# Banks of a product opened one by one, and queries and keys 2 and 3 made in one product

## The chip, the cores and the metric

The kernel runs on one core of one Trainium2 chip. The metric is the device time of one execution in microseconds. Three runs of the kernel before gave 1106.72 to 1108.7 us with a median of 1107.58 us; less is better.

## The reference

A trunk of two layers on 512 tokens of width 1024, in float32. Layer A mixes with trailing means, layer B with twelve heads of stick-breaking attention, and both have four memory heads beside that and a SwiGLU block behind. Layer B's queries, and the keys and values, are projections of the same x, with two different gains in front of the matrices.

```python
D_MODEL, SEQ, DEPTH = 1024, 512, 2            # BATCH = 1
HEAD_DIM, N_SB_HEADS, N_MEM_HEADS, MEM_TOKENS = 64, 12, 4, 256
D_FF, SB_BLOCK = 2816, 128

def stick_breaking_attention(q, k, v):
    ...
    for i in range(s // SB_BLOCK):
        ...
        z = jnp.einsum("bhqd,bhkd->bhqk", qb, kb).astype(jnp.float32) * scale
        mask = spos[None, :] < tpos[:, None]
        log_not = jnp.where(mask, jax.nn.log_sigmoid(-z), 0.0)
        later = lax.cumsum(log_not, axis=3, reverse=True) - log_not
        wts = jnp.where(mask, jnp.exp(jax.nn.log_sigmoid(z) + later), 0.0)
        outs.append(jnp.einsum("bhqk,bhkd->bhqd", wts.astype(vb.dtype), vb))

def pool_layer(x, mem, ...):                  # layer A
    proj = rmsnorm(x, norm_mix) @ w_in
    u_pool, q_mem = proj[..., :POOL_WIDTH], proj[..., POOL_WIDTH:]
    ...                                       # trailing means, grouped matmul
    mem_out = memory_attention(q_mem, mk, mv)
    x = x + jnp.concatenate([grouped, mem_out], axis=-1) @ w_out
    return x + swiglu(rmsnorm(x, norm_ffn), w_gu, w_down)

def sb_layer(x, mem, k_sh, v_sh, ...):        # layer B
    proj = rmsnorm(x, norm_mix) @ w_q         # 12 heads of queries, 4 memory heads
    ...
    sb_out = stick_breaking_attention(q_sb, k_sh, v_sh)...
    mk, mv = memory_kv(mem, mem_norm, w_mem_kv)
    mem_out = memory_attention(q_mem, mk, mv)
    x = x + jnp.concatenate([sb_out, mem_out], axis=-1) @ w_out
    return x + swiglu(rmsnorm(x, norm_ffn), w_gu, w_down)

# in reference(): before layer B
            kv = rmsnorm(x, kv_norm) @ w_kv   # keys and values from the same x, another gain
# at the end
    return rmsnorm(x, final_norm)
```

## The kernel before

**Tiles and products.** x stands as 8 tiles of 128 features by 512 tokens. Each float32 operand of a product is split in a high and a low part (h and l at the end of a name), and a product of two operands is three matmuls: low part with high, high with low, and high with high (`mm3`, L278 to L280). Weights are cut in bricks of 128 rows by up to 512 columns. SyncE loads two bricks with one transfer of 512 KB (names `wr_...`), into a ring of four. `wsplit` makes the high part on ScalarE (L223, or L227 with a gain) and the low part on VectorE (L224, or L228 with a gain); these too have a ring of four, and run two bricks ahead. A gain belongs to a range of columns, so a brick whose columns come from two matrices with different gains is split in as many pieces, each with its own instruction on either engine.

**Banks.** A product collects four outputs (n) of 128x512 in four banks of PSUM ("acc"); four more ("at") serve the attention heads. `product` runs the bricks (k) over the banks. `staggered` sets the order: brick by brick over all banks, and at the end, for the last two bricks (`STAGGER`), bank by bank, so that the banks close one after another. A bank opens when what read the product before out of it is done.

**Layer B's queries, keys and values.** They are made by five products, `b_qkv0` to `b_qkv4`, whose outputs `QKV_GROUPS` lists (L82): q 6 and 7 are the memory heads' queries, each other q or k holds two of the twelve heads, each v four heads. When a bank closes, `evac` in `qkv` reads it out. For a q, `stack_q` makes the high part (ScalarE, L237) and the low part (VectorE, L238), and four transfers on SyncE's queue (L505) bring them into the tiles `qs` that the scores read. For a k, VectorE first multiplies with the row scale (`qkf`, L978), ScalarE makes the high part (`hk`, L513), VectorE the low part (L514), and `dup_k` issues eight transfers. `qh`, `ql`, `qkf` and `hk` share one ring of four buffers (tag "hl"), so a fifth of them waits until the transfers that read the first are done. For a v, ScalarE (L551) and VectorE (L552) write it token by token.

**Attention.** A head and block of tokens starts with scores `zs` on TensorE (L610, L611), then two sigmoids on ScalarE (`nb`, `be`; L613, L614), masks on GpSimd (L615, L617), a scan (`it`, L620) and a multiplication (`be`, L622) on VectorE. TensorE transposes the weights (`tp`, L561), ScalarE and VectorE split them (`ath`, `atl`; L237, L238, or a copy on ScalarE alone for the later heads, L565), and TensorE multiplies with the values (`av`, L650). Memory heads run through `zm`, `pt` and the same transposes. A head can begin when its q and its k have been brought in place.

**What sets the order.** TensorE's order is written by hand by a planner in the program: it keeps a clock of its own, charges each engine for what it issues (`chain`, `COST`), notes when each tile will be there, and weaves pieces of heads between a product's steps where it expects them to be ready. The other engines' order follows from a scheduler that sees TensorE's. Each engine runs its instructions in order, so an instruction that waits holds up all that is behind it.

Of the kernel before, what the change touches and what calls it, by code (L numbers as in the profile page):

```python
# [59 lines left out]
STAGGER = 2  # L60
# [18 lines left out]
POOL_LEAD = 1.32  # L79
MAN_A = True  # L80
MAN_B = True
QKV_GROUPS = [[('q', 6), ('q', 7), ('q', 0), ('q', 1)], [('k', 0), ('k', 1), ('v', 0)], [('q', 2), ('q', 3), ('q', 4), ('q', 5)], [('k', 2), ('k', 3), ('v', 1)], [('k', 4), ('k', 5), ('v', 2)]]  # L82


def _plan():
# [3 lines left out]
    def ffn(l, g):  # L89
        out = []  # L90
        for (j0, j1), downs in PARTS[l]:
            for _ in range(j0, j1, 2):
                out.append((f"{l}_gu", k8, [(0, 512, g)]))
            for d0, d1 in downs:
                out += [(f"{l}_down", list(range(d0, d1)), None)] * 2
        if l == "b":
            out.append(("b_last", list(range(*LAST)) * 2, None))
        return out
# [11 lines left out]
    plan += ffn("a", G_AFFN)  # L110
    for gi, tiles in enumerate(QKV_GROUPS):
        cuts, c = [], 0
# [13 lines left out]
class Net:  # L126
# [85 lines left out]
    def wsplit(self, w, k, gains=None, stays=False):  # L212

        nc = self.nc
        cols = w.shape[-1]
        self.chain([("act", cols), ("dve", cols)] if gains is None else [("acts", cols), ("stt", cols)])
        if stays:
            wh, wl = self.t("xh", F32R), self.t("xl", F32R)
        else:
            wh = self.wp.tile([P, cols], F32R, tag="wh", name="wh", bufs=4)  # L220
            wl = self.wp.tile([P, cols], F32R, tag="wl", name="wl", bufs=4)
        if gains is None:
            nc.scalar.copy(wh, w)  # L223
            nc.vector.tensor_tensor(out=wl, in0=w, in1=wh.bitcast(F32), op=ALU.subtract)  # L224
        else:
            for c0, c1, g in gains:
                nc.scalar.activation(wh[:, c0:c1], w[:, c0:c1], AF.Copy, scale=self.gain(g, k))  # L227
                nc.vector.scalar_tensor_tensor(  # L228
                    out=wl[:, c0:c1], in0=w[:, c0:c1], scalar=self.gain(g, k),
                    in1=wh.bitcast(F32)[:, c0:c1], op0=ALU.mult, op1=ALU.subtract)  # L230
        return wh, wl
# [127 lines left out]
    def product(self, name, ks, nb, mul, evac, alone=False):  # L359

        ps = [self.any_ps("acc") if alone else self.ps("acc", "acc") for _ in range(nb)]
        w = {}
        for i, n in staggered(len(ks), nb):
            if i not in w:
                w[i] = self.next_brick(name)
            if i == 0 and not alone:
                self.until(self.accs.popleft())
            mul(ps[n], n, *w[i], ks[i], i == 0, i == len(ks) - 1)
            if i == len(ks) - 1:
                done = evac(n, ps[n])  # L370
                if not alone:
                    self.accs.append(done)
            yield
# [299 lines left out]

def staggered(nk, nb):

    for k in range(nk - STAGGER):
        for n in range(nb):
            yield k, n
    for n in range(nb):
        for k in range(nk - STAGGER, nk):  # L680
            yield k, n
# [8 lines left out]
def trunk_kernel(ctx: ExitStack, tc: tile.TileContext, a, out):  # L690
# [274 lines left out]
    def qkv(gi):  # L965
        tiles = QKV_GROUPS[gi]
        units = [u for u, (t, _) in enumerate(tiles) for _ in range(1 + (t == "v"))]
# [74 lines left out]
    with net.in_order() if MAN_B else ExitStack():  # L1042
        for gi in range(len(QKV_GROUPS)):
            net.weave(qkv(gi), ma, att)
# [80 lines left out]
```

## Time and profile before

| what | us |
|---|---|
| median of three runs | 1107.58 |
| the profiled execution | 1108.93 |
| its span | 1107.2 |
| TensorE busy | 1086.5 |
| VectorE busy | 679.2 |
| ScalarE busy | 498.4 |
| GpSimd busy | 77.1 |

The profile is taken from one execution. TensorE's busy time is the length of its matmuls, which overlap: one of 512 columns is listed with about 390 ns, and the next starts 0.23 us after it. So the end of a wait is read better from the starts of two neighbours than from the busy time. The chain that ended last is 90% TensorE's own instructions.

### The profile page before, as it was taken

What the parts mean: (1) busy time and instruction counts of PE and PEld (TensorE: products, weight loads), DVE (VectorE), ACT (ScalarE), POOL (GpSimd) and SP (SyncE); (2) the same over time, 40 slices, a digit from 0 to 9 for tenths busy, and PEclk for the clock granted to TensorE, in tenths of its full rate; (3) what the DMA queues carried; (4) which work ended last, traced back from release to release, by engine and by line L of the source; (5) the groups of instructions that cost most, each with busy time, mean ns of one, the idle gap of its engine ahead of it and who ended that gap; (6) DMA issues with size and microseconds to landing.
All of it is one profiled execution on the core that took longest, in us unless ns stands there. A gap on an engine that the chain in (4) does not pass through costs nothing.

```text
span 1107.2 us, 14396 instructions
## 1 busy us (share of the span) xinstructions
PE 1086.5 (98%) x5280; PEld 913.4 (82%) x5280; DVE 679.2 (61%) x1118; ACT 498.4 (45%) x911; POOL 77.1 (7%) x130
## 2 busy tenths in 40 slices
PE   9999999999999999999998999999999999999997
PEld 7997888888888888888877888788888888888887
DVE  7987876544444534565578799784653365444574
ACT  7557553332333323344786676553332243323343
POOL 0000040000000000000013133240000000000000
PEclk9999999999999999999999999999999999999998
DMA  7464222222222222223554433122222222222212
GB/s 269 141 198 122 76 96 95 95 95 95 96 97 104 99 100 96 95 95 102 145 135 125 124 110 107 52 85 87 95 104 104 96 96 96 96 95 95 96 57 77
DMA packets 39366, 117.48 MB, mean 106 GB/s; under 512 B 5120, under 2 KB 7168, under 8 KB 39296
## 3 DMA queue, kind: packets, MB, share of 16 engines
q1 hardware_dynamic: 39152, 116.54, 32.0%
q8 instruction: 41, 0.67, 0.2%
q14 instruction: 29, 0.24, 0.1%
q10 hardware_dynamic: 144, 0.03, 0.0%
HBM read 100.83 MB, written 2.10 MB: 93 GB/s over the span
## 4 chain that ended last, share of the span: by engine, by line
PE 90%; issue 4%; ACT 2%; DVE 1%; DMA 1%; POOL 1%; SPq 0%; POOLq 0%; DVEq 0%; ACTq 0%
PE acc L278 27%; PE acc L279 27%; PE acc L280 27%; PE av L650 2%; PE tp L561 1%; ACT pt L592 1%; DMA wr_a_in<-in_a_in_dram 1%; PE zs L610 1%; PE zs L611 1%; PE ps_ss L302 0%; PE last L278 0%; PE last L279 0%; DMA qs<-ql 0%; ACT wh L227 0%; POOL be L617 0%
## 5 line engine op out<-in xcount | busy, mean ns | idle before, releaser
L278 PE MATMUL acc<-xh,wh 128*128 128x512 f32 x880 | 342.9, 392 | 1.7 <-DVE vs L552 1.1
L279 PE MATMUL acc<-xl,wh 128*128 128x512 f32 x880 | 342.8, 390 | 0.0
L280 PE MATMUL acc<-xh,wl 128*128 128x512 f32 x880 | 341.8, 389 | 0.0
L278 PEld LDWEIGHTS acc<-xh,wh 128*128 128x128 f32 x880 | 165.6, 188 | 35.7 <-issue 1.5
L280 PEld LDWEIGHTS acc<-xh,wl 128*128 128x128 f32 x880 | 165.2, 188 | 34.6
L279 PEld LDWEIGHTS acc<-xl,wh 128*128 128x128 f32 x880 | 165.4, 188 | 32.9 <-DVE xl L238 0.2
L228 DVE SCALAR_TENSOR_TENSOR wl<-wr_a_gu,gains,wh 128x512 fp32r<-128x512 f32 x88 | 67.1, 766 | 105.7 <-ACT wh L227 105.7
L228 DVE SCALAR_TENSOR_TENSOR wl<-wr_b_gu,gains,wh 128x512 fp32r<-128x512 f32 x88 | 67.0, 762 | 105.6 <-ACT wh L227 105.6
L278 PE MATMUL acc<-hh,wh 128*128 128x512 f32 x320 | 124.5, 389 | 0.0
L279 PE MATMUL acc<-hl,wh 128*128 128x512 f32 x320 | 124.5, 389 | 0.0
L280 PE MATMUL acc<-hh,wl 128*128 128x512 f32 x320 | 124.3, 389 | 0.0
L227 ACT ACTIVATE wh<-wr_b_gu,gains 128x512 fp32r<-128x512 f32 x88 | 63.6, 724 | 133.5 <-PE acc L279 105.5
L227 ACT ACTIVATE wh<-wr_a_gu,gains 128x512 fp32r<-128x512 f32 x88 | 63.3, 724 | 133.3 <-PE acc L279 107.3
L278 PEld LDWEIGHTS acc<-hh,wh 128*128 128x128 f32 x320 | 60.1, 188 | 12.5
L280 PEld LDWEIGHTS acc<-hh,wl 128*128 128x128 f32 x320 | 60.1, 188 | 12.5
L279 PEld LDWEIGHTS acc<-hl,wh 128*128 128x128 f32 x320 | 60.1, 188 | 12.4
L224 DVE TENSOR_TENSOR wl<-wr_a_down,wh 128x512 fp32r<-128x512 f32 x44 | 30.4, 690 | 60.1 <-ACT wh L223 49.9
L223 ACT CAST wh<-wr_a_down 128x512 fp32r<-128x512 f32 x44 | 27.4, 622 | 72.6 <-PE acc L279 67.9
L307 POOL TENSOR_TENSOR rs<-var,mhalf 128x4 f32<-128x4 f32 (+1 forms) x7 | 6.6, 942 | 756.1 <-DVE var L305 756.1
L224 DVE TENSOR_TENSOR wl<-wr_b_down,wh 128x512 fp32r<-128x512 f32 x36 | 24.9, 690 | 49.1 <-ACT wh L223 40.9
L278 PE MATMUL acc<-mixh,wh 128*128 128x512 f32 x128 | 51.6, 403 | 2.8 <-DVE mixl L860 1.5
L279 PE MATMUL acc<-mixl,wh 128*128 128x512 f32 x128 | 50.2, 392 | 0.2 <-DVE mixl L1020 0.2
(204 smaller groups left out, 1691.4 us busy)
## 6 DMA issues: line engine op xcount, KB each, us to landing
wr_a_gu<-in_a_gu_dram SPq DMA_DIRECT2D x44, 512.0 KB, 3.5
wr_b_gu<-in_b_gu_dram SPq DMA_DIRECT2D x44, 512.0 KB, 3.5
wr_a_down<-in_a_down_dram SPq DMA_DIRECT2D x22, 512.0 KB, 3.5
wr_b_qkv<-in_b_qkv_dram SPq DMA_DIRECT2D x20, 512.0 KB, 3.6
wr_b_down<-in_b_down_dram SPq DMA_DIRECT2D x18, 512.0 KB, 3.5
wr_a_out<-in_a_out_dram SPq DMA_DIRECT2D x8, 512.0 KB, 3.5
wr_b_out<-in_b_out_dram SPq DMA_DIRECT2D x8, 512.0 KB, 3.6
wr_a_in<-in_a_in_dram SPq DMA_DIRECT2D x7, 512.0 KB, 4.0
```

Of the source, the lines that this page charges most:

```text
L223: nc.scalar.copy(wh, w)
L224: nc.vector.tensor_tensor(out=wl, in0=w, in1=wh.bitcast(F32), op=ALU.subtract)
L227: nc.scalar.activation(wh[:, c0:c1], w[:, c0:c1], AF.Copy, scale=self.gain(g, k))
L228: nc.vector.scalar_tensor_tensor(out=wl[:, c0:c1], in0=w[:, c0:c1], scalar=self.gain(g, k), in1=wh.bitcast(F32)[:, c0:c1], op0=ALU.mult, o ...
L278: mm(ps, wh, xh, start=first, stop=False)
L279: mm(ps, wh, xl, start=False, stop=False)
L280: mm(ps, wl, xh, start=False, stop=last)
L561: nc.tensor.transpose(tp[:, i * P:(i + 1) * P], blk, self.ident)
L592: nc.scalar.activation(pt[:, b], z[:, b], AF.Exp, scale=sp[:, 2 * pr + i:2 * pr + i + 1], bias=mx[:, i:i + 1], accum_out=sm[:, i:i + 1])
L610: nc.tensor.matmul(z[:, :end], q, kh[:, :end], start=True, stop=False)
L611: nc.tensor.matmul(z[:, :end], q, kl[:, :end], start=False, stop=True)
L650: self.nc.tensor.matmul(to, vv, part, start=ia == 0 and i == 0, stop=ia == nu - 1 and i == len(parts) - 1)
```

## The change

`QKV_GROUPS` puts k 2 and 3 with q 2 and 3 in the third product, and q 4 and 5 with v 1 in the fourth. `wsplit` charges the planner's clock for each piece of a brick. `staggered` begins a product of more than four bricks (`2 * STAGGER`) bank by bank with the first two bricks, in the way in which it ended before. This holds for both layers' input products but the very first of the program, the q, k and v products, and the longer part of each output product; the SwiGLU block has an order of its own.

```diff
--- before.py
+++ after.py
@@ -79,7 +79,7 @@
 POOL_LEAD = 1.32
 MAN_A = True
 MAN_B = True
-QKV_GROUPS = [[('q', 6), ('q', 7), ('q', 0), ('q', 1)], [('k', 0), ('k', 1), ('v', 0)], [('q', 2), ('q', 3), ('q', 4), ('q', 5)], [('k', 2), ('k', 3), ('v', 1)], [('k', 4), ('k', 5), ('v', 2)]]
+QKV_GROUPS = [[('q', 6), ('q', 7), ('q', 0), ('q', 1)], [('k', 0), ('k', 1), ('v', 0)], [('q', 2), ('q', 3), ('k', 2), ('k', 3)], [('q', 4), ('q', 5), ('v', 1)], [('k', 4), ('k', 5), ('v', 2)]]
 
 
 def _plan():
@@ -213,7 +213,8 @@
 
         nc = self.nc
         cols = w.shape[-1]
-        self.chain([("act", cols), ("dve", cols)] if gains is None else [("acts", cols), ("stt", cols)])
+        for n in [None] if gains is None else [c1 - c0 for c0, c1, _ in gains]:
+            self.chain([("act", cols), ("dve", cols)] if n is None else [("acts", n), ("stt", n)])
         if stays:
             wh, wl = self.t("xh", F32R), self.t("xl", F32R)
         else:
@@ -673,7 +674,11 @@
 
 def staggered(nk, nb):
 
-    for k in range(nk - STAGGER):
+    first = STAGGER if nk > 2 * STAGGER else 0
+    for n in range(nb):
+        for k in range(first):
+            yield k, n
+    for k in range(first, nk - STAGGER):
         for n in range(nb):
             yield k, n
     for n in range(nb):
```

Bricks of the third and of the fourth product now have columns of two gains, so ScalarE runs 898 instructions in place of 882 in its listing and VectorE 1136 in place of 1120; TensorE, GpSimd and SyncE have as many as before.

Below are pieces of the order of instructions before and after, with the number of a tile or buffer behind its name; the lines of the changed file are one higher from L214 on, and five higher from L679 on.

TensorE at the opening of the third product. `acc_4970` to `acc_4973` are its four banks before, `acc_4974` to `acc_4977` after; `wh_4818` is brick 0, `wh_4843` and `wh_4845` brick 1. Of each step of three matmuls the first stands here. Before:

```order
L278 MATMUL acc_4970<-xh_4200,wh_4818 128x512
...
L561 MATMUL tp_4998<-ident_69,pt_4789 128x128 x2
...
L278 MATMUL acc_4971<-xh_4200,wh_4818 128x512
...
L278 MATMUL acc_4972<-xh_4200,wh_4818 128x512
...
L278 MATMUL acc_4973<-xh_4200,wh_4818 128x512
...
L278 MATMUL acc_4970<-xh_4207,wh_4843 128x512
...
L278 MATMUL acc_4971<-xh_4207,wh_4843 128x512
```

After:

```order
L279 MATMUL acc_4974<-xh_4200,wh_4818 128x512
...
L279 MATMUL acc_4974<-xh_4207,wh_4845 128x512
...
L562 MATMUL tp_5013<-ident_69,pt_4789 128x128 x2
...
L279 MATMUL acc_4975<-xh_4200,wh_4818 128x512
...
L279 MATMUL acc_4975<-xh_4207,wh_4845 128x512
...
L279 MATMUL acc_4976<-xh_4200,wh_4818 128x512
...
L279 MATMUL acc_4976<-xh_4207,wh_4845 128x512
...
L279 MATMUL acc_4977<-xh_4200,wh_4818 128x512
```

Banks 1, 2 and 3 open one, two and three steps later, and brick 1 is read by the second step in place of the fifth.

VectorE where the third product's outputs are read out. Before, `ql_5310` and `ql_5340` are the low parts of q3 and q4, and `atl_5387` is a slice of attention weights that TensorE's `zs` at 595.20 us came behind:

```order
L238 TENSOR_TENSOR ql_5310<-acc_4971,qh_5309 128x512
L622 TENSOR_TENSOR be_5295<-be_5295,it_5303 128x511
L620 SCALAR_TENSOR_TENSOR it_5330<-nb_5323 128x128
L238 TENSOR_TENSOR ql_5340<-acc_4972,qh_5339 128x512
L228 SCALAR_TENSOR_TENSOR wl_5372<-wr_b_qkv3_1_5369,gains_67,wh_5371 128x512
L622 TENSOR_TENSOR be_5322<-be_5322,it_5330 128x127
L228 SCALAR_TENSOR_TENSOR wl_5440<-wr_b_qkv3_1_5369,gains_67,wh_5439 128x512
L238 TENSOR_TENSOR atl_5387<-tp_5383,ath_5386 128x256
```

After, `qkf_5345` is k2 times the row scale, and `atl_5325` is the next slice:

```order
L239 TENSOR_TENSOR atl_5317<-tp_5311,ath_5316 128x512
L983 TENSOR_TENSOR qkf_5345<-acc_4976,rb_4509 128x512
L621 SCALAR_TENSOR_TENSOR it_5339<-nb_5332 128x512
L239 TENSOR_TENSOR atl_5325<-tp_5320,ath_5324 128x384
L229 SCALAR_TENSOR_TENSOR wl_5408<-wr_b_qkv3_1_5405,gains_67,wh_5407 128x256 x2
L623 TENSOR_TENSOR be_5331<-be_5331,it_5339 128x511
```

The row that needs the first buffer of the ring a second time is now a multiplication on VectorE, ahead of the scan and of the slice, and the weight splits are two halves each.

ScalarE in the same place. Before, `qh_5339` and `qh_5355` are the high parts of q4 and q5, `ath_5386` the high part of the slice:

```order
L237 CAST qh_5339<-acc_4972 128x512
L227 ACTIVATE wh_5371<-wr_b_qkv3_1_5369,gains_67 128x512
L227 ACTIVATE wh_5439<-wr_b_qkv3_1_5369,gains_67 128x512
L237 CAST qh_5355<-acc_4973 128x512
L237 CAST ath_5386<-tp_5383 128x256
```

After, `hk_5347` is k2's high part, and `ath_5324` and `ath_5436` are slices:

```order
L238 CAST ath_5324<-tp_5320 128x384
L228 ACTIVATE wh_5407<-wr_b_qkv3_1_5405,gains_67 128x256 x2
L614 ACTIVATE nb_5370<-zs_5366,sn_4476 128x128
...
L228 ACTIVATE wh_5416<-wr_b_qkv3_1_5405,gains_67 128x256 x2
L514 CAST hk_5347<-qkf_5345 128x512
L238 CAST ath_5436<-tp_5433 128x256
```

The weight splits now stand ahead of the row that waits for a buffer, and one slice does too.

## Rows read from the trace of the kernel before

**Rows 1.** The page, part 1: busy us (share of span) xinstructions, by engine.
```profile
PE 1086.5 (98%) x5280; PEld 913.4 (82%) x5280; DVE 679.2 (61%) x1118; ACT 498.4 (45%) x911; POOL 77.1 (7%) x130
```

**Rows 2.** TensorE's waits, 526.5 to 727.7 us: total us, times, longest us.
```profile
PE zs L610 <- DVE atl L238: 3.1, 1, 3.1
PE acc L278 <- DVE vs L552: 2.4, 3, 1.1
PE av L650 <- ACT ath L565: 1.2, 3, 0.4
```

**Rows 3.** Windows by stage: length, busy us of PE, PEld, DVE, ACT, POOL, PEclk, DMA, GB/s.
```profile
526.50:727.70 201.20, 192.04 (x1090) 163.70 (x1089) 161.13 (x277) 140.40 (x303) 49.24 (x98) 0.99 0.40 109
575.00:600.00 25.00, 21.94 (x113) 18.86 (x112) 21.80 (x36) 17.38 (x36) 8.06 (x18) 0.93 0.48 127
665.00:710.00 45.00, 45.00 (x229) 37.13 (x228) 43.09 (x73) 30.97 (x68) 16.75 (x34) 1.00 0.30 93
```

**Rows 4.** TensorE's timeline, 589 to 599 us: start, length, instruction [idle before <-releaser].
```profile
591.52 0.40 PE L279 MATMUL acc<-xl,wh 128*128 128x512 f32 x1
591.75 0.39 PE L280 MATMUL acc<-xh,wl 128*128 128x512 f32 x1
595.20 0.69 PE L610 MATMUL zs<-kh,qs 128*128 128x384 f32 x1 [3.06 <-DVE atl L238]
...
596.00 0.41 PE L278 MATMUL acc<-wh,xh 128*128 128x256 f32 x1
...
597.92 0.40 PE L278 MATMUL acc<-wh,xh 128*128 128x256 f32 x1
```

**Rows 5.** ScalarE's timeline, 588 to 596 us.
```profile
591.42 0.59 ACT L237 CAST qh<-acc 128x512 fp32r<-128x512 f32 x1 [2.82 <-DMA qs<-qh]
```

**Rows 6.** VectorE's timeline, 584 to 597 us.
```profile
588.86 1.21 DVE L620 TENSOR_TENSOR_SCAN it<-nb 128x512 f32<-128x512 f32 x1
...
592.60 0.69 DVE L238 TENSOR_TENSOR ql<-acc,qh 128x512 fp32r<-128x512 f32 x1 [1.01 <-DMA qs<-ql]
...
594.73 0.42 DVE L238 TENSOR_TENSOR atl<-tp,ath 128x256 fp32r<-128x256 f32 x1
```

**Rows 7.** Transfers into qs: whole q/k/v stage first, then 575 to 600 us.
```profile
DMA to landing us min/median/max: 2.2/2.4/4.9
...
DMA to landing us min/median/max: 2.3/3.9/4.9
```

**Rows 8.** TensorE's timeline at seven waits, 87 to 93.5 and 527.8 to 632 us.
```profile
89.63 0.50 PE L278 MATMUL acc<-mixh,wh 128*128 128x512 f32 x1 [1.50 <-DVE mixl L860]
...
92.94 0.47 PE L278 MATMUL acc<-mixh,wh 128*128 128x512 f32 x1 [0.30 <-DVE v_b_mem L552]
...
529.88 0.39 PE L278 MATMUL acc<-wh,xh 128*128 128x256 f32 x1 [0.53 <-DVE ql L238]
...
559.35 0.72 PE L561 MATMUL tp<-ident,pt 128*128 128x128 f32 x2 [0.38 <-ACT pt L597]
...
562.55 0.47 PE L278 MATMUL acc<-xh,wh 128*128 128x512 f32 x1 [1.08 <-DVE vs L552]
...
629.89 0.35 PE L278 MATMUL acc<-wh,xh 128*128 128x256 f32 x1 [1.02 <-DVE vs L552]
...
631.32 0.36 PE L278 MATMUL acc<-wh,xh 128*128 128x256 f32 x1 [0.30 <-DVE vs L552]
```

**Rows 9.** ScalarE's timeline, 527 to 541 us.
```profile
530.90 0.72 ACT L227 ACTIVATE wh<-wr_b_qkv,gains 128x512 fp32r<-128x512 f32 x1
531.64 1.28 ACT L592 ACT_TABLE_LOAD   x1
```

**Rows 10.** The chain of waits, 705 to 727.7 us: start us, us, what.
```profile
712.35 0.38 ACT ath L565
```

**Rows 11.** VectorE's groups by form, 526.5 to 727.7 us.
```profile
L622 DVE TENSOR_TENSOR be<-be,it 128x511 f32<-128x511 f32 x12 | 8.6, 717 | 0.7
...
L622 DVE TENSOR_TENSOR be<-be,it 128x255 f32<-128x255 f32 x12 | 5.2, 431 | 0.7
```

## The prediction

> **What bounds the kernel now.** I read the page's busy shares first. TensorE is busy for 98% of the span [rows 1], and both kernels give it the same matmuls, so the only thing a reordering can change is the time in which TensorE stands still between them. The second view is the list of TensorE's waits in the stage that the regrouping touches, layer B's five q/k/v products with the attention heads woven into them (526.5 to 727.7 us). Its largest entries are one wait of 3.1 us for an attention slice split by VectorE, three waits of 2.4 us together for value tiles, and three of 1.2 us for copies of attention weights [rows 2]. The third view, the table by stage, shows what stands beside TensorE there: VectorE busy 161 of 201 us, ScalarE 140, and in 665 to 710 us VectorE at 43.09 of 45.00 while TensorE never waits [rows 3]. VectorE is thus a near second bound.
>
> The fourth view is the timeline around the long wait. Matmuls of 512 columns are issued 0.23 us apart; the last before the wait starts at 591.75 and the next instruction at 595.20 [rows 4]. That is 3.22 us lost beyond the issue rate, against the 3.06 us of idle that the view prints, so a gap costs the printed idle plus some 0.16 us. I use that for all gaps below. From 595.20 to 598.14 TensorE then runs at half rate: matmuls of 256 columns last 0.41 us, from 596.00 to 597.92 (ten of them) [rows 4], and the granted clock of the 25 us is 0.93 where the stages beside it show 1.00 [rows 3]. Half of those 2.94 us, 1.5 us, is the price of the lower of the two clock levels (1.2 against 2.4 GHz). The wait and its tail cost 4.7 us.
>
> Why VectorE was late stands in the timelines of ScalarE and VectorE. ScalarE's high part of the third bank (q4) waited 2.82 us for the transfer that reads q2's high part [rows 5]; VectorE's low part waited 1.01 us for q2's low part until 592.60, two weight splits and a multiplication then stood ahead of the slice, and it ran at 594.73 [rows 6]. The four buffers that hold q parts are all used by q2 and q3, so q4 and q5 must wait for their transfers. Such transfers land 2.4 us after issue in the middle over the stage, 3.9 us in these 25 us and 4.9 us at most [rows 7].
>
> **The change part by part.** *Bank by bank opening.* With eight or six or five bricks in a product, banks now take bricks 0 and 1 each before the next bank opens. Bank 1 opens one step of three matmuls later (3 x 0.23 = 0.69 us), bank 2 two steps (1.4 us), bank 3 three steps (2.1 us), so what empties the banks has that much more time. In exchange brick 1 is wanted three steps earlier.
>
> In layer A's stage, the bank that waited 0.30 us (0.46 with the issue slot) for a value tile is now reached later, and that wait goes. The 1.50 us wait ahead of it ends with ScalarE's row of softmax work, which doesn't move [rows 8]. Gain 0.5 us, bounds 0 and 0.8.
>
> At the second product, the wait of 0.53 us (0.69) for q0's low part goes [rows 8]. But the third brick's high part, 0.72 us, which ran just ahead of ScalarE's table load of 1.28 us, now comes behind the load and the first two exponentials [rows 9]. The row of softmax work that the next transposes wait for ends some 0.5 us later by that, and as TensorE arrives 0.69 us earlier, its wait there grows by both. Net a loss of 0.5 us; bounds a loss of 1.2 (the whole brick and half a table load late) and a gain of 0.7.
>
> At the third product, the fourth bank's wait of 1.08 us (1.24) for a value tile goes: with 2.1 us more, TensorE comes after the tile. The transposes ahead of it, which waited 0.38 us (0.54, and some 0.3 more inside the pair of two, which took 0.72) [rows 8], find TensorE one step later and keep about 0.4 us. Gain 1.7 us, bounds 1.2 and 2.1.
>
> At the last product the two waits of 1.02 and 0.30 us (1.18 and 0.46) for value tile 1 go [rows 8], because TensorE reaches these two banks 1.4 and 2.1 us later, and that is more than either wait. Gain 1.6 us, bounds 1.2 and 1.6.
>
> *Regrouping.* Product 3 ends in q2, q3, k2, k3. The parts of k2 and k3 go through the same four buffers as those of q, so the buffer wait doesn't vanish. It changes engines: VectorE's product of k2 with the row scale is now the first to want q2's buffer, where ScalarE's high part of q4 was. ScalarE no longer has 2.82 us of waiting in front of two weight splits and of the attention slices behind it. But VectorE's row cannot start before the 591.42 us at which ScalarE was released [rows 5], and behind it stand a scan of 512 columns (1.21 us) and the slice that TensorE wants: 0.69 us for the product, as for a low part of that size, 1.21 for the scan and some 0.55 for a slice of 384 columns, which lies above the 0.42 of 256 [rows 6]. So it is ready at 593.9, and TensorE, whose order has about 1.0 us of matmuls more ahead of it than what ended at 591.8, is there at about 592.8: a wait of 1.1 us in the better case, and perhaps 1.05 and 0.2 us more at the next two heads. I take 1.8 us in place of 4.7 with no fall of the clock after it: gain 2.9 us, bounds 0 (the wait is only moved) and 4.7. The last head's scores also stand nine matmuls (2.0 us) earlier in TensorE's order, which removes one of the three waits of 0.4 us for copies of attention weights [rows 2] before the last products' bricks, the chain's row at 712.35 [rows 10]: gain 0.6, bounds 0 and 0.9.
>
> *Pieces.* Products 3 and 4 now both mix q with k or v columns, so each of 16 bricks is split in two halves of 256 columns on ScalarE and on VectorE. By the multiplications of two lengths (717 ns for 511 columns, 431 ns for 255) [rows 11] an instruction costs 146 ns beside its 1.12 ns a column. Sixteen more are 2.3 us of VectorE's time. They lie beside other work, since VectorE idles 40 of the 201 us [rows 3]; if all of them were on the path it would be 2.3 us. I take 0.3 us, near the covered end, because TensorE didn't wait even where VectorE stood at 96% [rows 3].
>
> The Trainium skill speaks against this part: "VectorE: DVE Perf Modes", section "The TRN2 errata", says that every instruction from SBUF pays a fixed latency and that tiles should stay at 512 elements or more. Its measured 151 cycles at 0.96 GHz would make 16 x 157 ns = 2.5 us, an estimate close to the 2.3 us that the two rows give, so by that rule nothing in the sum changes unless the cover is gone.
>
> The sum: 0.5 - 0.5 + 1.7 + 1.6 + 2.9 + 0.6 - 0.3 = 6.5 us saved. The profiled execution took 1108.93 us, its span of 1107.2 and 1.7 around it; less 6.5 us that is 1102.4. The median of the runs shown is 1.35 us lower, 1107.58, so the time to expect is 1101.1 us. The edit of the weight split's cost in the planner runs nothing on the chip; it only shapes the order.
>
> **The rivals.** *The buffer wait only moves.* k2's parts need the same buffers as q4's. For it speaks that transfers in these 25 us take up to 4.9 us to land [rows 7] and that the slices queue behind the waiting row. Against it, ScalarE's two weight splits and its slices are free of it. The 4.7 us stay, and the other terms give 3.6 us: 1104.0.
>
> The Trainium skill would leave less room for this rival: "DMA: Bandwidth & Descriptors", section "Anatomy of one DMA", gives some 2.0 us fixed and the bytes at 436 GB/s, 2.3 us for these 128 KB, an estimate. The stage's median of 2.4 us agrees and the 3.9 us of this stretch [rows 7] doesn't; by the page's figure the buffers would be free before TensorE asks, the whole 4.7 us would go and the time be 1.8 us lower than the forecast, 1099.3.
>
> *Slower: VectorE's queue sets the pace.* Its new waiting row at about 591 holds all that follows on VectorE, where the old wait cost VectorE only 1.01 us [rows 6]. If VectorE idles there for the 2.82 us that ScalarE did [rows 5], it loses 1.8 us more than now, and the halves take 2.3 us: 4.1 us later from there on. What TensorE waits for at the later openings and in the tail (value tiles, slices, low parts) is nearly all VectorE's, so the gains there are given back, the 4.7 us of the old wait and its lower clock come back in their old size, and only layer A's 0.5 us stay: 3.6 us slower, 1111.2. For it speak the 43.09 of 45.00 us [rows 3], which leave no room to catch up; against it, that TensorE took those 45 us without a wait. It decides from the point at which VectorE is later than its idle time in 575 to 600 us, 3.2 us (21.80 busy of 25.00) [rows 3], can take up.
>
> *No difference.* The openings' waits were short because ScalarE or VectorE was late by its own queue; what TensorE saves at an opening it waits for at the next head. For it speaks the loss at the second product, against it that the three value-tile waits have no later customer within 2 us. Then within 2 us of 1107.6.
>
> *More.* All the waits but the tail's go, and the clock never falls: the upper bounds add to 10.1 us, 1097.5 or somewhat less.
>
> **How the numbers follow.** The forecast holds with 0.52 (1098 to 1105 its own range), the moved wait with 0.20 (1104), no difference 0.11, slower 0.09, more 0.08. A change of 0.2%, 2.2 us, is the least that can be told from none here. Faster: 0.52 + 0.20 + 0.08 = 0.80; same 0.11; slower 0.09. The range that leaves out the better 0.08 and the slower 0.12 (slower, and a part of no difference) is 1097 to 1108.
>
> **What would show it.** Right: in the changed profile no wait at the fourth bank of the third product or at the last product for value tiles; the wait for an attention slice near 590 us no longer than 2 us; a granted clock of 1.00 in 575 to 600 us. Wrong: a wait of about 3 us for a slice behind VectorE's k2 row; VectorE idle on a transfer for over 2 us there; waits above 1 us in 665 to 710 us, where there are none now; or the second product's transposes waiting 3 us.

## The result and the profile after

The changed kernel took 1100.95 us in the median of four runs (1100.38 to 1103.6) beside 1107.82 of the kernel before in the same sessions: a ratio of 0.9939 with a 95% interval of 0.9927 to 0.995. A second measurement in another session gave 0.9927 (0.9913 to 0.994). The forecast was 1101.1. The profiled execution took 1101.17 us, its span 1099.4, so 7.8 us less than before on either count.

The page's first part: busy us (share of the span) and instructions of each engine.

```profile
PE 1083.6 (99%) x5280; PEld 911.8 (83%) x5280; DVE 678.7 (62%) x1134; ACT 500.0 (45%) x927; POOL 80.4 (7%) x130
```

TensorE has the same 5280 matmuls; its busy time is 2.9 us less [rows 1]. A matmul at the lower clock is listed longer, one of 256 columns with 0.41 us [rows 4] instead of 0.28, which goes that way. TensorE's waits in the q/k/v stage (total us, times, longest):

```profile
PE tp L562 <- ACT pt L598: 1.4, 1, 1.4
PE av L651 <- ACT ath L566: 0.8, 2, 0.4
PE acc L279 <- ACT mixh L1024: 0.7, 1, 0.7
PE av L651 <- DVE atl L239: 0.4, 1, 0.4
```

The 3.1 us for a slice and the 2.4 us for value tiles [rows 2] are gone. What stands at the head is new: 1.4 us for softmax weights, at the second product. The windows by stage (length, busy us of PE, PEld, DVE, ACT, POOL, then PEclk, DMA share, GB/s), the first one from the same start to the stage's end, whose last wait ends at 719.10 us where it ended at 726.85:

```profile
526.50:721.00 194.50, 190.56 (x1097) 163.96 (x1096) 162.41 (x295) 143.00 (x320) 53.35 (x99) 1.00 0.41 116
575.00:600.00 25.00, 24.58 (x143) 21.40 (x141) 23.30 (x45) 20.56 (x46) 7.50 (x17) 1.00 0.53 138
665.00:710.00 45.00, 44.19 (x217) 35.26 (x216) 38.99 (x63) 27.67 (x61) 16.64 (x28) 1.00 0.22 77
```

VectorE is no less busy than before [rows 3], and TensorE stands still less. In 575 to 600 us the granted clock is 1.00. TensorE's timeline there (start, length, instruction, [idle before <- releaser]):

```profile
591.22 0.33 PE L651 MATMUL av<-ath,vs 128*128 128x384 f32 x1
591.98 0.45 PE L651 MATMUL av<-atl,vs 128*128 128x384 f32 x1 [0.42 <-DVE atl L239]
```

The wait of 3.06 us [rows 4] has become one of 0.42 (0.58 by the starts, 591.22 to 591.98 less 0.18 for a matmul of 384 columns). VectorE's and ScalarE's timelines show why:

```profile
589.66 0.68 DVE L983 TENSOR_TENSOR qkf<-acc,rb 128x512 f32<-128x512 f32 x1
590.26 1.21 DVE L621 TENSOR_TENSOR_SCAN it<-nb 128x512 f32<-128x512 f32 x1
591.39 0.53 DVE L239 TENSOR_TENSOR atl<-tp,ath 128x384 fp32r<-128x384 f32 x1
```

```profile
590.61 0.67 ACT L514 CAST hk<-qkf 128x512 fp32r<-128x512 f32 x1
592.73 0.54 ACT L238 CAST ath<-tp 128x256 fp32r<-128x256 f32 x2 [1.45 <-PE tp L562]
```

VectorE multiplied k2 with the row scale at 589.66, with no wait for a buffer, and ScalarE's high part followed at once; ScalarE's later slice at 592.73 waited for TensorE, not TensorE for it. In before, ScalarE stood until 591.42 at this point [rows 5]. The transfers of these 25 us, issue to landing:

```profile
DMA to landing us min/median/max: 2.3/2.9/4.6
```

The middle one takes 2.9 us, not 3.9 [rows 7].

To see where the time went I add up, over all of TensorE's matmuls, by how much the step from one start to the next exceeds the issue rate for its columns (0.227 us for 512, 0.174 for 384, 0.120 for 256, 0.11 for 128). Lost us by stretch, for the profiled execution of each kernel:

| stretch, us | before | opening alone | regrouping alone | regrouping, late openings | both (after) |
|---|---|---|---|---|---|
| 500 to 550 | 1.7 | 2.3 | 1.7 | 1.8 | 2.2 |
| 550 to 575 | 2.4 | 0.4 | 2.8 | 2.8 | 0.8 |
| 575 to 600 | 4.8 | 4.5 | 3.0 | 0.4 | 0.9 |
| 600 to 650 | 2.7 | 1.3 | 4.7 | 1.2 | 0.4 |
| 650 to 750 | 8.5 | 10.8 | 7.1 | 7.7 | 7.5 |
| all five | 20.0 | 19.2 | 19.3 | 13.9 | 11.7 |
| the rest of the kernel | 8.5 | 8.5 | 8.2 | 8.2 | 9.0 |

The three columns in the middle are experiments, told below. From before to after, 8.3 us go in the five stretches and 0.5 come back elsewhere, 7.8 in all, which is the difference of the two spans.

### The profile page after: what moved, and what is told of

Read it like the earlier page. It is cut to its first block, busy times and chain, and to the rows that moved or that the text cites. A ratio compares the mean times of both kernels' runs of the same rounds, so it can differ in the third digit from the quotient of the medians.

```text
span 1099.4 us, 14436 instructions
## 1 busy us (share of the span) xinstructions
PE 1083.6 (99%) x5280; PEld 911.8 (83%) x5280; DVE 678.7 (62%) x1134; ACT 500.0 (45%) x927; POOL 80.4 (7%) x130
## 4 chain that ended last, share of the span: by engine, by line
PE 54%; issue 40%; DVE 3%; DMA 1%; POOL 0%; ACT 0%; SPq 0%; POOLq 0%; DVEq 0%; ACTq 0%
PE acc L279 15%; PE acc L280 15%; PE acc L281 15%; PE av L651 2%; PE tp L562 1%; DVE wl L229 1%; DMA wr_a_in<-in_a_in_dram 1%; PE zs L612 1%; PE zs L611 1%; DVE xl L239 1%; PE last L279 0%; PE last L280 0%; PE last L281 0%; DVE x L771 0%; PE acck L279 0%
```

## The experiments

The question is which of the two edits gives which part, and whether the buffers behind q and k are the cause of the long wait. The theory says that each edit removes waits of its own; the rivals say that one of them does it all, or that VectorE's queue decides.

**Opening alone.** The regrouping and the planner's charge left out:

```diff
+    first = STAGGER if nk > 2 * STAGGER else 0
+    for n in range(nb):
+        for k in range(first):
+            yield k, n
-    for k in range(nk - STAGGER):
+    for k in range(first, nk - STAGGER):
```

> The kernel before with the opening bank by bank alone; the products are grouped as before (q2 to q5 in the third). Theory: the two edits remove different waits, the opening those for value tiles and the first row of layer A, the grouping the one for a buffer that transfers read. Then the openings give some 3.2 us (0.6 in layer A, a loss of 0.6 at the second product, 1.6 at the third, 1.6 at the last), the wait of about 3 us for an attention slice near 590 us stays, and the time is about 1104.6. Rival: the later openings give the transfers the time that they need, so that the wait goes here too; then 1101 to 1102.

Measured: 1105.82 us beside 1108.55, ratio 0.9979 (0.9968 to 0.9991). The waits for value tiles went, and the long wait stayed, as the theory has it. TensorE's timeline, and the window around it:

```profile
591.81 0.39 PE L280 MATMUL acc<-xh,wl 128*128 128x512 f32 x1
594.86 0.44 PE L610 MATMUL zs<-kh,qs 128*128 128x384 f32 x1 [2.66 <-ACT be L614]
...
595.31 0.28 PE L278 MATMUL acc<-wh,xh 128*128 128x256 f32 x1
595.43 0.28 PE L279 MATMUL acc<-wl,xh 128*128 128x256 f32 x1
...
595.90 0.39 PE L280 MATMUL acc<-wh,xl 128*128 128x256 f32 x1
596.09 0.41 PE L278 MATMUL acc<-wh,xh 128*128 128x256 f32 x1
596.30 0.41 PE L279 MATMUL acc<-wl,xh 128*128 128x256 f32 x1
```

```profile
575.00:600.00 25.00, 22.34 (x116) 19.39 (x114) 20.86 (x35) 16.49 (x35) 9.66 (x18) 0.93 0.47 126
```

2.82 us are lost between 591.81 and 594.86, though q2's parts were cast and sent some 2 us earlier than before: the later openings alone don't free the buffers, and their transfers take up to 6.3 us to land. ScalarE's `be`, which ends the wait, stands behind two high parts of q that waited 2.3 and 0.8 us for buffers; ahead of the first the profile names TensorE, but the transfer out of its buffer landed at 590.44 and it began at 590.54. The matmuls that follow start 0.12 us apart at first and 0.21 us apart from 595.90 to 599.29, which is the lower clock level. The gain is 2.3 us in place of 3.2. The profiled execution loses 2.3 us more than before in 650 to 750 us; it took 1107.97 us, 2.2 more than the median, so it is not shown that this is what the others lack.

**Regrouping alone.** `QKV_GROUPS` and the charge as in the changed kernel, `staggered` as before.

> The kernel before with the regrouping and the planner's charge for pieces, the openings as before (brick by brick). Theory: the wait near 590 us falls from 4.7 us with its lower clock to under 1 us, the tail gains 0.9, and the waits for value tiles at the third and the last product stay, so about 4.5 us less than before, 1103.3. Rival: without the later openings VectorE has more due at once, its row of k2 waits for the transfers as ScalarE's of q4 did, and the time is 1106 to 1108.

Measured: 1108.12 us beside 1108.55, ratio 0.9995 (0.9986 to 1.0004): no difference to be told. This is the rival's time. TensorE's timeline at the fourth and at the fifth product, and VectorE's row of k3:

```profile
593.14 0.39 PE L611 MATMUL zs<-kh,qs 128*128 128x256 f32 x1 [0.89 <-ACT be L615]
...
594.85 0.39 PE L279 MATMUL acc<-wh,xh 128*128 128x256 f32 x1 [0.49 <-DVE qkf L979]
...
597.09 0.38 PE L651 MATMUL av<-atl,vs 128*128 128x256 f32 x1 [0.45 <-DVE atl L239]
```

```profile
633.80 0.55 PE L279 MATMUL acc<-wh,xh 128*128 128x256 f32 x1 [2.47 <-DVE vs L553]
...
634.37 0.42 PE L281 MATMUL acc<-wh,xl 128*128 128x256 f32 x1
634.58 0.41 PE L279 MATMUL acc<-wh,xh 128*128 128x256 f32 x1
```

```profile
594.11 0.68 DVE L979 TENSOR_TENSOR qkf<-acc,rb 128x512 f32<-128x512 f32 x1
```

The one long wait is now three short ones. The second of them shows the link between the edits: the fourth product opens its last bank at 594.85 behind VectorE's read-out of k3, which had only started at 594.11. And at the fifth product the bank that v1 is read out of cost 2.47 us of waiting where it had been 1.02 [rows 8], with a stretch at the lower clock level behind it (0.93 in 625 to 650 us). Whether VectorE waited for a transfer, as the rival had it, is another matter: the rows of k2 (590.21) and k3 stand in a stretch in which VectorE is busy without a gap, so it was its queue.

**Regrouping with late openings.** To test that link, bank by bank in the fourth and fifth product alone:

```diff
-        for i, n in staggered(len(ks), nb):
+        for i, n in staggered(len(ks), nb, name in ("b_qkv3", "b_qkv4")):
...
-def staggered(nk, nb):
+def staggered(nk, nb, opens=True):
...
-    first = STAGGER if nk > 2 * STAGGER else 0
+    first = STAGGER if opens and nk > 2 * STAGGER else 0
```

> The regrouping with only the fourth and the fifth product opened bank by bank, the first three products and layer A and the output products as before. Theory: regrouping alone gained nothing since the fourth product's banks, opened brick by brick, wait for VectorE's read-out of k2 and k3, and the fifth's for v1 (2.95 and 4.09 us lost in 575 to 600 and 625 to 650 us); bank by bank there, these fall to about 1 and 0.1, and the time is 1103 to 1104, ratio 0.9955. Rival: it is the earlier openings that make room for VectorE, and the ratio stays at 0.999.

Measured: 1102.64 us beside 1108.56, ratio 0.9945 (0.9933 to 0.9958), so the theory's side. TensorE's waits in 526 to 730 us, and the windows:

```profile
PE acc L279 <- DVE vs L553: 1.1, 1, 1.1
PE tp L562 <- ACT pt L598: 0.7, 1, 0.7
PE acc L279 <- ACT mixh L1024: 0.7, 1, 0.7
PE zs L611 <- DVE ob L574: 0.6, 1, 0.6
```

```profile
575.00:600.00 25.00, 25.00 (x141) 21.50 (x140) 22.15 (x42) 19.63 (x45) 7.24 (x16) 1.00 0.49 132
625.00:650.00 25.00, 25.00 (x169) 23.07 (x168) 24.07 (x44) 19.02 (x44) 10.12 (x21) 1.00 0.24 73
```

In 575 to 600 us TensorE lost 0.4 us where regrouping alone lost 3.0, and in 625 to 650 it never stood. The one wait for a value tile that is left is that of the third product, which still opens as before. So the regrouping and the two late openings together give 6.1 us, where regrouping alone gave nothing that can be told. How much of it the two openings would give without the regrouping was not run; in the run with all the openings alone, 600 to 650 us lost 1.4 us less than before.

**Six buffers for the parts of q and k, before's order of products.** Their room is taken from the weight buffers, so both runs have three of these instead of four, one with four buffers for q and k (the control) and one with six. TensorE's 5280 matmuls come in the same order in both.

```diff
-NRAW = 4
-SLOTS = {..., "hl": 4, ...}
+NRAW = 3
+SLOTS = {..., "hl": 6, ...}
```

> The kernel before with three weight buffers of 512 KB in place of four: the control for the run with six q and k buffers, which needs their room. Both theories: the wait near 590 us for a slice behind q4's parts stays at about 3 us with its lower clock; a buffer less may delay weights by up to 2 us in all, 1107.5 to 1110.

> The same with six buffers for the parts of q and k instead of four. Theory: q4's parts waited for the transfers out of q2's buffers; with two more they don't, the wait near 590 us falls under 1 us, the clock stays up, and the time is 3 to 4.5 us less than the control's. Rival: the buffers are not what holds the slice, VectorE has as much due ahead of it anyway, and the time is within 1 us of the control's with the wait in the same place.

Measured: 1108.8 us, ratio 0.9998 (0.9987 to 1.0008), for the control, and 1105.19 us, ratio 0.9964 (0.9951 to 0.9977), with six: 3.6 us less with two buffers more. TensorE's waits in 575 to 600 us, and the window, of the control, and then the wait with six:

```profile
PE zs L610 <- DVE atl L238: 2.7, 1, 2.7
```

```profile
575.00:600.00 25.00, 22.26 (x124) 19.07 (x123) 21.88 (x37) 18.54 (x38) 7.66 (x18) 1.00 0.50 128
```

```profile
PE zs L610 <- ACT be L614: 1.0, 1, 1.0
```

The buffers are what held the slice. The wait doesn't vanish, though: 1.0 us is left, now behind ScalarE. The lower clock, which both expectations gave to the control, is not in its profile (1.00). The wait of 0.53 us for q0's low part [rows 8] is gone too, since q0 and q1 went through the same four buffers.

**Four pieces in place of two.** The changed kernel with every half split once more, its order of TensorE kept:

```diff
+            if len(gains) == 2:
+                gains = [(c, c + P, g) for c0, c1, g in gains for c in range(c0, c1, P)]
             for c0, c1, g in gains:
```

> The changed kernel with the bricks of products 3 and 4 split in four pieces of 128 columns instead of two of 256, the planner's order of TensorE the same: 32 more instructions on ScalarE and on VectorE. Theory: they lie beside TensorE's work, so 0 to 0.6 us more, 1101 to 1101.6. Rival: VectorE sets the pace of this stage; then 32 x 0.146 us, 4.7 us more, 1105.6, with waits for slices and value tiles from 575 us on.

Measured: 1103.54 us, ratio 0.9955 (0.9941 to 0.9969), against 0.9939 and 0.9927 of the changed kernel: 1.8 to 3.1 us for 32 more instructions on each engine, 0.06 to 0.10 us each. Neither theory: between covered and paid in full. TensorE's timeline shows the two places that pay:

```profile
564.94 0.47 PE L281 MATMUL acc<-xh,wh 128*128 128x512 f32 x1 [1.48 <-DVE vs L555]
...
592.82 0.45 PE L653 MATMUL av<-atl,vs 128*128 128x384 f32 x1 [0.42 <-DVE atl L241]
...
602.07 0.50 PE L613 MATMUL zs<-kh,qs 128*128 128x512 f32 x1 [0.91 <-DVE ob L576]
```

The value tile of the third product (1.48 us) and an output of a head (0.91 us) come late; the slice between them waits as in the changed kernel.

**The second product opened as before** in the otherwise changed kernel, where TensorE waits 1.4 us for softmax weights:

```diff
-        for i, n in staggered(len(ks), nb):
+        for i, n in staggered(len(ks), nb, name != "b_qkv1"):
```

> The changed kernel with the second q/k/v product alone opened brick by brick as before. Theory: the loss at that product (1.5 us of waiting for softmax weights in place of 0.5, less 0.7 of waiting for q0's low part) goes, 0.6 us less, 1100.3. Rival: TensorE, earlier by 0.6 us, meets the same late tiles at the next opening and the time is that of the changed kernel, 1101.

Measured: 1100.51 us, ratio 0.9923 (0.9909 to 0.9937), not to be told from the changed kernel. In its trace the wait for softmax weights is gone, and two others stand there:

```profile
528.74 0.36 PE L585 MATMUL zm<-kdb,qs 128*128 128x256 f32 x1 [0.41 <-DMA qs<-ql]
...
530.68 0.38 PE L279 MATMUL acc<-wh,xh 128*128 128x256 f32 x1 [0.52 <-DVE ql L239]
```

The loss in 500 to 575 us is 3.0 us in both. The rival's time holds, though TensorE meets the wait at this product and not at the next opening. That the transfers of the first product's q set this place fits the combination with six buffers below, in which that loss halves.

**The old charge of the planner**, in the otherwise changed kernel:

> The changed kernel with the old charge in the planner, one piece a brick, though the bricks of products 3 and 4 are still split in two. Theory: the charge moves a few heads' pieces by a step and is worth at most 0.5 us, 1101 to 1101.5. Rival: without it TensorE's order meets the halves too early and waits for weight parts in products 3 and 4, 1103.

Measured: 1103.04 us, ratio 0.9943 (0.9928 to 0.9958). The interval overlaps that of the changed kernel, so the time settles nothing. It is the rival's time, but TensorE waits for no weight parts in the trace. That trace, of one execution, has something that the changed kernel has not, a wait of ScalarE's for a buffer and behind it 1.5 us of TensorE's for the row of k3:

```profile
ACT hk L513 <- DMA qs<-ql: 2.0, 1, 2.0
ACT hk L513 <- DVE qkf L982: 2.0, 1, 2.0
```

```profile
PE acc L278 <- DVE qkf L982: 1.5, 1, 1.5
```

So with another order from the planner the buffers bind again in this execution; the size of it, 0 to 2 us, stays open.

**q 4 and 5 in the last product**, k 4 and 5 in the fourth, on top of the run with the second product opened as before:

```diff
-QKV_GROUPS = [..., [('q', 4), ('q', 5), ('v', 1)], [('k', 4), ('k', 5), ('v', 2)]]
+QKV_GROUPS = [..., [('k', 4), ('k', 5), ('v', 1)], [('q', 4), ('q', 5), ('v', 2)]]
```

> The changed kernel with the second product opened as before, and with k 4 and 5 beside v 1 in the fourth product and q 4 and 5 beside v 2 in the last. Theory: a q is read out with two parts and four transfers, a k with a product, two parts and eight transfers, so the last four heads start 2 us earlier in the order and the tail's waits (5.2 us of lost time in 700 to 725 us) shrink by 1 to 2: 1099. Rival: the tail hangs on the last heads' own chain of scan, copies and values, not on their start, and the time stays at 1100.5.

Measured: 1101.17 us, ratio 0.9928 (0.9914 to 0.9943): no gain. 650 to 750 us lose 8.1 us against 7.5. The last transfer of q and k parts was issued at 655.27 us in place of about 664, so the last heads could have begun earlier, but the last scores began at 701.61 in place of 698.50. So the run doesn't test what an earlier start of these heads is worth; it shows that parts in place sooner did not bring one.

**The changed kernel again, and the two that pointed further together**: the second product as before, with six buffers and three weight buffers.

> The changed kernel once more, beside the next two on the same chip: 0.9939 of the kernel before, within 0.001.

> The changed kernel with the second product opened as before, six buffers for the parts of q and k and three weight buffers in place of four. Theory: what is left of the waits for buffers at the first product's read-out (0.6 and 0.7 us near 528 and 530 us) goes, no wait for transfers was left near 590 us: 1.0 to 1.5 us less than with four buffers, some 0.992 to 0.9915 of the kernel before. Rival: that time is met again as a wait for softmax weights at the next transposes (they end with ScalarE's own row), and the ratio is 0.9935.

Measured: 1100.6 us, ratio 0.9927 (0.9913 to 0.994), for the changed kernel, 0.0012 below the 0.9939 that was expected within 0.001, and 1099.16 us, ratio 0.9918 (0.9903 to 0.9933), for the combination. The median of the combination is the lowest of all, but the intervals overlap, so it is not shown to be faster. In its profiled execution 500 to 575 us lose 1.5 us instead of 3.2 for the changed kernel beside it, and the end of the stage gives it back (650 to 750 us lose 10.2 us against 7.5), in part at the lower clock:

```profile
700.00:725.00 25.00, 21.88 (x91) 16.69 (x90) 16.95 (x22) 11.19 (x23) 4.28 (x3) 0.93 0.16 49
```

## Why the prediction came out

The time was met (1101.1 forecast, 1100.95), the mechanism in its parts less well than the sum. That the two agree to 0.15 us is luck: the profiled executions differ by 7.8 us where the sum has 6.5, and the medians of the second measurement by 8.0. The upper bounds of the prediction add to 10.8 us, not 10.1, as the 0.7 of the second product is left out there.

- *Openings.* Third product: 1.7 us forecast, 1.6 measured (2.4 lost before, 0.8 after). First two products: a loss of 0.5 forecast, 0.5 measured, and by the wait that was named, for softmax weights, which is 1.36 us of idle after:

```profile
540.21 1.16 PE L562 MATMUL tp<-ident,pt 128*128 128x128 f32 x6 [1.36 <-ACT pt L598]
```

- Fourth and fifth product: 1.6 forecast, 2.3 measured; two waits of 0.2 to 0.3 us ahead of scores, which the forecast left out, went as well. Layer A: 0.5 forecast, 0.6 gained in 75 to 100 us (2.4 lost before, 1.8 after). The wait of 1.50 us there stayed at 1.44, as forecast, but the row names VectorE's `mixl` as what ends it [rows 8], not ScalarE's softmax work. Yet all that lies outside the stage lost 0.5 us more than before with this gain counted in; 0.4 of that is the first 25 us, which vary by themselves (3.6 to 5.0 us lost in the runs here).
- *The long wait.* The sum had 2.9 us for it, and 3.9 were measured. The step that failed is the one that bound VectorE's row: "VectorE's row cannot start before the 591.42 us at which ScalarE was released". It ran at 589.66. That bound took the transfers' landing as given, but their issue follows the order too: the two transfers of q2's high part left SyncE's queue at 584.46 and 585.01 in place of 585.72 and 586.62 and landed at 589.0 and 589.4 in place of 590.7 and 591.3. Their time in flight matters too: with the openings alone the two left earlier still, at 583.61 and 584.17, and the second landed only at 590.4. What sets that time is not shown. That the buffers were the cause was right, as the run with six shows.
- *What the sum could not show* is that the terms belong together. It added the regrouping's 3.2 us (2.9 and 0.6 less 0.3) to the openings' 3.3. Alone they gave 0.5 and 2.3 us; together 6.8 to 8.1. The later openings are worth more after the regrouping, since by then the banks of k3 and v1 are what VectorE is late for.
- *Pieces.* The 2.3 us of VectorE's time hold: the 32 halves are busy for 14.2 us after, where 16 wholes at 0.75 us (14 of them take 10.5) would be busy for 12.0, so 2.2 us more. The listed lengths of 476 and 755 ns overlap their neighbours. The 0.3 us on the path was too low by the run with quarters, which puts 0.06 to 0.10 us of each added instruction there. Carried to 16 instructions that is 0.9 to 1.6 us, an estimate. VectorE's groups by form, 526.5 to 721 us, then two halves after and a whole before, each with no idle behind it (the row after the whole starts at 594.73 [rows 6]):

```profile
L229 DVE SCALAR_TENSOR_TENSOR wl<-wr_b_qkv,gains,wh 128x256 fp32r<-128x256 f32 x32 | 14.2, 476 | 1.0 <-ACT wh L228 1.0
...
L229 DVE SCALAR_TENSOR_TENSOR wl<-wr_b_qkv,gains,wh 128x512 fp32r<-128x512 f32 x14 | 10.5, 755 | 4.2 <-ACT wh L228 4.2
```

```profile
591.84 0.87 DVE L229 SCALAR_TENSOR_TENSOR wl<-wr_b_qkv,gains,wh 128x256 fp32r<-128x256 f32 x2
592.63 0.68 DVE L623 TENSOR_TENSOR be<-be,it 128x511 f32<-128x511 f32 x1
```

```profile
594.06 0.75 DVE L228 SCALAR_TENSOR_TENSOR wl<-wr_b_qkv,gains,wh 128x512 fp32r<-128x512 f32 x1
```

- The rule of "VectorE: DVE Perf Modes" in the Trainium skill, section "The TRN2 errata", spoke against this part and was right in direction: by the starts two halves take 0.79 us and the whole 0.67, so 0.12 us more, somewhat less than the 157 ns, an estimate, that its 151 cycles make. The gain elsewhere was larger.
- *The rivals.* "The buffer wait only moves" would have left 4.7 us near 590 us; 575 to 600 us lose 0.9 after. Regrouping alone gained as little as if the wait had only moved, but its waits were for rows of ScalarE and VectorE and not for transfers. The case in which the buffers are free before they are wanted (1099.3) is the nearest in its mechanism: VectorE's row of k2 ran without a wait and 3.9 of the 4.7 us went, though the transfers took 2.9 us in the middle. The fit behind the prediction's estimate of 2.3 us, in the Trainium skill under "DMA: Bandwidth & Descriptors", section "Anatomy of one DMA", is given there for transfers that GpSimd issues, while SyncE issues these. "Slower" found its place (VectorE's row of k3, the value tile of v1) in regrouping alone, but only to no difference. The tail gained 1.0 us against 0.6.

## What to carry to other kernels

Price an edit of the order together with the others that move the same engine's queue: here regrouping alone gave nothing that can be told, the openings alone 2.3 us, and both 6.8 to 8.1. A wait for a buffer is best shown by giving it another buffer, at the price of a control for the memory taken elsewhere. And a time at which a transfer landed is no bound for another order, since the order sets when it is issued.

## What the runs showed that was not expected

Whether the clock falls is not told by the length of a wait. In the profiles 3.06 us of idle in before [rows 4], 2.66 with the openings alone and 2.47 with regrouping alone each have a stretch of matmuls at half rate behind them; it begins with the first matmul in before and 1.0 us after the wait with the openings alone. In the control with three weight buffers 2.7 us of idle leave the window at 1.00. And in the combination's profile the window of 700 to 725 us shows 0.93 with no wait over 1 us in its first 18 us.

The same kernel can differ in this from one execution to the next. The profiles with such a stretch have a mean granted clock of 0.995 or 0.996 over the whole execution, all others 0.997 or 0.998. Sorted by that, 15 of the 23 executions of before that were measured beside the openings alone have one (1109.4 us in the mean, the other eight 1107.2), but only 3 of the 12 with the openings alone and 1 of the 9 of the changed kernel. The control has one in 8 of 10, the run with six buffers in 1 of 5. So part of what the medians show as gained is the clock, which falls less often: beside each other, at 0.997 and above, before takes 1107.6 us (three executions) and the changed kernel 1100.8 (five), 6.9 us apart where the medians are 8.0 apart, and the openings alone gain 1.5 us (1107.2 to 1105.7). The mean clock has the end of the program in it too, so the sorting is a reading and not a proof. The 1.5 us that the forecast gave to the clock are thus the price where it falls, and not a price of every wait of 3 us.

A weight buffer of 512 KB less cost nothing that can be told (0.9998).
